# Attention outputs of two sets of tokens, instead of two partial sums, in the row halves of a tile

## The chip, the cores and the metric

The kernel runs on one core of a Trainium2 chip. The metric is the device time of one launch in microseconds (us), as the median of several runs. The engines of the core run side by side, each through its own instructions in order: TensorE (PE) for matmuls and transposes, VectorE (DVE), ScalarE (ACT), GpSimd (POOL), and SyncE (SP), which here only issues DMAs.

## The reference

One decoder layer runs over a prompt of 2048 tokens and, with the same weights, over 32 sample tokens. All is float32; the model has 1024 channels, 8 attention heads of 64 channels and as many channels (512) in a spatial gate.

```python
q, k, v, u, vg = _project(x, norm1_g, w_in)            # RMSNorm, one projection
for (w, d), bias_hj in zip(BRANCHES, biases):          # (128,1), (512,4), (2048,16)
    o, l = _dilated_prompt(q, k, v, bias_hj, d, w // d + 1)
    outs.append(o); lses.append(l)
att = _merge_branches(outs, lses).reshape(B, S, D_ATT) # softmax over the branches' sums
...
x = x + jnp.concatenate([att, u * gate], axis=-1) @ w_out
x = x + _swiglu(x, norm2_g, w_gate, w_up, w_down)      # RMSNorm, SwiGLU
```

A query sees keys at distances 0 to 128, at multiples of 4 up to 512, and at multiples of 16 up to 2048, each with a bias by distance; the three results are weighted per token and head by their softmax sums. Outputs are the new hidden states (after one more RMSNorm) and the key, value and gate caches.

## The kernel before

**Stages.** From the start of the span: the first projection with the gate and the sample's attention (to about 600 us), the prompt's attention head by head (600 to 960), a tail in which the last head's end meets the output projection of the first block (950 to 1100), then the feed-forward part for three blocks of 6, 6 and 4 token tiles of 128, of which each begins with its output projection and second norm (blocks 1 and 2 near 1640 and 2240).

**A head.** The first two branches are one banded attention: 16 query tiles, each against up to five key tiles (`band_scores`, L864; minimum and bias on DVE, L870; exp on ACT, L875; transposes, L891). Four query tiles are a group G. `band_values` multiplies the group's weights with the values. For each of the up to eight key tiles one matmul serves all query tiles that see it, up to 512 columns; an output has only the head's 64 channels, so matmuls go in turn to the upper and the lower 64 rows of a PSUM bank. Upper and lower rows thus hold two partial sums of the same tokens. `band_out` copies them to `ob` (128 x 512). The third branch works on tokens of equal remainder mod 16, four remainders at a time: POOL puts k and the two parts of q in that order (`strided_order`, L937), scores L945, softmax L950 to L960, transposes L965, values L974 (64 rows, 128 columns per remainder) and copies to `o3` (L981).

**Statistics and merge.** `Stats` turns the minima and sums of a head into two factors per token (L998 to L1028, small DVE operations and a matmul, L1004) and stores them to DRAM (`f_d`). `merge_load` brings a chunk of 512 tokens of both factors to all partitions. `merge` then multiplies the band result by the first factor (L1054), the strided one by the second (L1056) and adds the strided one to the upper rows (L1058); there are four chunks per head, nearly all on POOL, one on DVE. `merge_store` writes the upper rows to `cat_d` and the lower rows to a second place of it.

**Output projection.** `load_cat` loads a token tile: eight slices of 128 channels (gate and first partial sums) and four slices of second partial sums. `split_cat` adds the two (L1335) and splits the result in a rounded part (ACT, L1338) and the rest (DVE, L1339); `out_part` multiplies both with split weights (L1347 to L1349, 12 matmuls per half unit). `second_end` adds the last half to the residual and starts the second norm: `norm2_a` squares, `norm2_b` makes the root and the normalised tile (L1400), `norm2_c` transposes it (L1414, eight transposes into two PSUM tiles) and copies out rounded parts, rests and sums of quarters (L1422 to L1434), the operands of the feed-forward products (L1553 to L1555).

**Order of the work.** Every engine runs in the order in which the program is written. In attention a `Plan` table of steps and phases sets it. From the output projection on there are ticks: a half unit (12 matmuls) or a product is one tick, and `later(n, f)` calls `f` n ticks on. `norm2_b` comes two ticks after `norm2_a`, `norm2_c` three ticks plus `put_off` after that.

Of the kernel before, what the change touches and what calls it, by code (L numbers as in the profile page):

```python
# [19 lines left out]
P = 128  # L20
T = 2048
# [43 lines left out]
def hymba_step(ctx: ExitStack, tc: tile.TileContext, A: dict, O: dict):  # L65
# [46 lines left out]
    cat_d = dram.tile([D + DA, T], F32, name="cat_d")  # L112
# [791 lines left out]
    def band_values(it, part):  # L904

        grp, d, G = it["grp"], it["d"], it["n"] // 4
        if part == 0:
            grp["o"] = bank(3)
        o = grp["o"]
        order = [i for i in (4, 3, 5, 2, 6, 1, 7, 0) if 4 * G - 4 + i >= 0]  # L910
        L = len(order)
        for x in range(part * L // 2, (part + 1) * L // 2):
            i = order[x]
            j0, j1 = max(0, i - 4), min(3, i)
            rows = slice(x % 2 * C, x % 2 * C + C)
            pe.matmul(o[rows, j0 * P:(j1 + 1) * P].rearrange("p (a b) -> p a b", b=P), d["vb"][:, 4 * G - 4 + i, d["z"], :],
                      grp["p"][:, 16 - 4 * i + 5 * j0:16 - 4 * i + 5 * j1 + 1:5, :], start=(x < 2), stop=(x >= L - 2))

    def band_out(it):
# [3 lines left out]
        dst, o = obs[h][:, G * 512:(G + 1) * 512], it["grp"]["o"]  # L923
        if G == 0:

            pool.memset(dst[C:P, 0:P], 0.0)
            act.activation(dst[0:C], o[0:C], AF.Copy)
            act.activation(dst[C:P, P:512], o[C:P, P:512], AF.Copy)
        else:
            act.activation(dst, o, AF.Copy)  # L930
# [38 lines left out]
    def strided_values(it):  # L969
        d, r4 = it["d"], it["n"]  # L970
        it["o"] = o = bank(3)
        for a in (0, 2, 1, 3):
            sl = slice(a * P, (a + 1) * P)
            pe.matmul(o[a // 2 * C:a // 2 * C + C, sl], d["vp"][:, r4 * 4 + a, d["z"], :], it["eT"][:, sl], start=True, stop=True)  # L974

    def strided_out(it):
        r4, h = it["n"], it["h"]
        if r4 == 0:
            o3s[h] = rp.tile([P, NT, P], F32, name="o3", tag="wide", bufs=2)
        for z in range(2):  # L980
            act.activation(o3s[h][0:C, r4 * 4 + z * 2:r4 * 4 + z * 2 + 2, :],  # L981
                           it["o"][z * C:(z + 1) * C, z * 256:(z + 1) * 256].rearrange("p (r i) -> p r i", r=2), AF.Copy)
# [54 lines left out]
    def merge_load(h, ch):  # L1037

        if h < H - 2 or h == H - 2 and ch < 2:
            f = pair_tile(F32)  # L1040
            mf[h, ch] = (f[:, 0], f[:, 1])
            act.dma_start(f, dap(f_d, h * 2 * T + ch * 512, [[0, P], [T, 2], [1, 512]]))
            return
        mf[h, ch] = (raw_tile(), zn_tile())
        for z, t_ in enumerate(mf[h, ch]):
            sync.dma_start(t_, dap(f_d, (h * 2 + z) * T + ch * 512, [[0, P], [1, 512]]))

    def merge(h, ch, eng, part=None):
        f1, f3 = mf[h, ch]
        x = obs[h][:, ch * 512:(ch + 1) * 512]  # L1050
        y = o3s[h][0:C].rearrange("p r i -> p i r")[:, ch * 32:(ch + 1) * 32, :]
        by_token = lambda v: v[0:C].rearrange("p (i r) -> p i r", r=NT)
# [7 lines left out]
    def merge_store(h, c0, c1):  # L1060
        for z in range(2):
            r0 = DA * (z + 1) + h * C
            sync.dma_start(cat_d[r0:r0 + C, c0 * 512:c1 * 512], obs[h][z * C:(z + 1) * C, c0 * 512:c1 * 512])
# [257 lines left out]
    def load_cat(B, i, a, b, place=None):  # L1321
# [4 lines left out]
        m = max(a, 4)  # L1326
        for dst, r0, n in ((cl[:, a:b], a * P, b - a), (ch[:, m:b], D + (m - 4) * P, b - m)):
            sync.dma_start(dst.bitcast(F32), cat_d[r0:r0 + n * P, t0:t0 + P].rearrange("(s p) t -> p s t", p=P))
        B.late[i] = (ch, cl, a, b)

    def split_cat(B, i, staged=raw_tile):
        ch, cl, a, b = B.late.pop(i)
        m = max(a, 4)
        x = staged()[:, 0:(b - m) * P].rearrange("p (s t) -> p s t", t=P)
        dve.tensor_add(x, cl[:, m:b].bitcast(F32), ch[:, m:b].bitcast(F32))  # L1335
# [715 lines left out]
```

## Time and profile before

| | |
|---|---|
| median of 3 runs | 2692.8 us (2679.7 to 2697.14) |
| profiled execution | 2691.25 us, span 2689.5 us, mean granted clock 0.967 |
| busy share of the span | PE 94%, DVE 51%, ACT 45%, POOL 52% |
| DMA | 468.45 MB, mean 174 GB/s |
| PE busy 800 to 850 us (a stretch of heads) | 44.03 us of 50 |
| PE busy 880 to 948 us (the last head) | 58.55 of 68 |
| PE busy 948 to 1000 us (the tail) | 36.94 of 52, granted clock 0.80 |

A line of the profile has a place in the code (L916), an engine, an operation and the tiles it writes and reads; what stands behind `<-` after an idle time is the instruction that ended it. "x8" joins eight instructions that follow each other; a float32 matmul counts twice, as it passes its columns twice. PEld is the loading of a matmul's stationary operand.

### The profile page before, as it was taken

To read this page: it belongs to the slowest core of one execution; us is meant where nothing else is said; L and a number is where in the kernel's file an instruction comes from. 1 tells how busy PE (TensorE), PEld (TensorE's weight loads), DVE (VectorE), ACT (ScalarE), POOL (GpSimd) and SP (SyncE) were. 2 spreads that over 40 slices of the span, in tenths; PEclk is the share of its full clock that TensorE was granted. 3 is DMA by queue.
4 is the path that set the end of the run, shared out by engine and by line. 5 is a ranking of instruction groups with operands and counts; after the bars stand their busy time and mean duration, and the time that the engine had idled before them with its cause. 6 is when DMAs were issued, how large, how long until landed. Compare 5 with 4: busy or idle time off the path is not lost. (4 is left out here: it accounts for less than half of the span.)

```text
span 2689.5 us, 38648 instructions
## 1 busy us (share of the span) xinstructions
PE 2533.0 (94%) x13578; PEld 2170.3 (81%) x13578; DVE 1375.7 (51%) x2724; ACT 1206.2 (45%) x2569; POOL 1408.6 (52%) x1048
## 2 busy tenths in 40 slices
PE   8998999999898877999999999999999998999997
PEld 6777777676665656999999987999999987999996
DVE  3268784436666664444444465444444455444445
ACT  6423344436666636545454545433232335433333
POOL 1036553224868753767676743545363533666663
PEclk9999999999999988899999999899999999899998
DMA  8765854675556374446364554436364543555653
GB/s 245 218 201 153 258 142 134 183 252 178 171 165 201 100 209 133 141 140 205 129 200 153 176 180 153 161 129 219 126 206 147 193 158 122 172 202 197 205 198 114
DMA packets 298165, 468.45 MB, mean 174 GB/s; under 512 B 26839, under 2 KB 163208, under 8 KB 292084
## 3 DMA queue, kind: packets, MB, share of 16 engines
q1 hardware_dynamic: 283588, 443.31, 51.4%
q10 hardware_dynamic: 14384, 22.68, 3.2%
q8 instruction: 108, 1.77, 0.3%
q14 instruction: 85, 0.70, 0.1%
HBM read 374.38 MB, written 161.64 MB: 199 GB/s over the span
## 5 line engine op out<-in xcount | busy, mean ns | idle before, releaser
L1496 POOL TENSOR_TENSOR op<-fr,op 128x512 fp32r<-128x512 f32 x385 | 489.1, 1300 | 318.5 <-ACT op L1492 297.2
L1553 PE MATMUL ps_m<-xh,op 128*128 128x384 f32 (+4 forms) x1932 | 629.6, 326 | 8.4 <-ACT xh L1430 5.3
L1554 PE MATMUL ps_m<-xl,op 128*128 128x384 f32 (+4 forms) x1932 | 627.8, 325 | 7.0 <-DVE xl L1433 7.0
L1555 PE MATMUL ps_m<-xh,op 128*128 128x384 f32 (+4 forms) x1932 | 627.5, 325 | 0.0
L1626 PE MATMUL ps_o<-dw,hw 128*128 128x512 f32 x2040 | 484.1, 392 | 9.3 <-DVE acc L1628 9.3
L1626 PEld LDWEIGHTS ps_o<-dw,hw 128*128 128x128 f32 x2040 | 379.7, 188 | 91.6 <-DVE acc L1628 16.0
L1553 PEld LDWEIGHTS ps_m<-xh,op 128*128 128x128 f32 x1932 | 377.4, 195 | 13.6 <-ACT xh L1430 5.9
L1554 PEld LDWEIGHTS ps_m<-xl,op 128*128 128x128 f32 x1932 | 377.9, 196 | 11.7 <-DVE xl L1433 7.7
L1555 PEld LDWEIGHTS ps_m<-xh,op 128*128 128x128 f32 x1932 | 377.1, 195 | 0.0
L1628 DVE TENSOR_TENSOR acc<-acc,ps_o 128x512 f32<-128x512 f32 (+1 forms) x362 | 247.0, 686 | 213.8 <-PE ps_o L1626 213.7
L1593 ACT ACTIVATE ps_t<-zn 128x384 f32<-128x384 f32 (+1 forms) x126 | 58.3, 463 | 480.5 <-DVE zn L1576 371.0
L1492 ACT ACTIVATE op<-fr 128x512 fp32r<-128x512 f32 x396 | 235.8, 622 | 21.1 <-DMA fr<-ab_d 17.7
L137 POOL TENSOR_TENSOR dw<-fd,dw 128x1024 fp32r<-128x1024 f32 x66 | 158.7, 2405 | 123.4 <-ACT dw L134 123.4
L317 PE MATMUL ps_s<-wh,xh 128*128 128x512 f32 x480 | 197.7, 412 | 6.4 <-ACT xh L134 6.1
L318 PE MATMUL ps_s<-wl,xh 128*128 128x512 f32 x480 | 191.9, 400 | 0.8 <-DVE wl L225 0.8
L319 PE MATMUL ps_s<-wh,xl 128*128 128x512 f32 x480 | 191.5, 399 | 0.0
L1496 POOL TENSOR_TENSOR op<-pair,op 128x512 fp32r<-128x512 f32 x63 | 81.4, 1298 | 117.3 <-ACT op L1492 117.3
L1603 ACT ACTIVATE hw<-ps_t 128x384 fp32r<-128x384 f32 (+1 forms) x126 | 56.1, 453 | 176.7 <-DVE ps_t L1599 175.8
L317 PEld LDWEIGHTS ps_s<-wh,xh 128*128 128x128 f32 x480 | 92.7, 193 | 36.2 <-issue 8.2
L603 POOL TENSOR_TENSOR vl<-kv,vh 100x512 fp32r<-100x512 f32 (+1 forms) x32 | 45.6, 1426 | 124.1 <-ACT vh L597 41.7
L319 PEld LDWEIGHTS ps_s<-wh,xl 128*128 128x128 f32 x480 | 92.5, 193 | 20.7 <-DVE xl L137 0.2
L318 PEld LDWEIGHTS ps_s<-wl,xh 128*128 128x128 f32 x480 | 93.1, 194 | 19.3 <-DVE wl L225 2.0
(451 smaller groups left out, 4575.5 us busy)
## 6 DMA issues: line engine op xcount, KB each, us to landing
fr<-ab_d SPq DMA_DIRECT2D x308, 256.0 KB
fd<-in_w_down_dram SPq DMA_DIRECT2D x66, 512.0 KB
out_ks_dram<-in_cache_k_dram SPq DMA_DIRECT2D x56, 512.0 KB
out_vs_dram<-in_cache_v_dram SPq DMA_DIRECT2D x56, 512.0 KB
ab_d<-fr SPq DMA_DIRECT2D x88, 256.0 KB
raw<-in_w_in_dram SPq DMA_DIRECT2D x72, 256.0 KB
qk_d<-pair SPq DMA_DIRECT2D x64, 256.0 KB
ab_d<-pair SPq DMA_DIRECT2D x63, 256.0 KB
```

The lines of the kernel that those rows point to most:

```text
L137: (eng_lo or pool).tensor_sub(lo, src, hi.bitcast(F32))
L317: pe.matmul(o[j], xh[:, k, :], wh, start=(k == 0), stop=False)
L318: pe.matmul(o[j], xh[:, k, :], wl, start=False, stop=False)
L319: pe.matmul(o[j], xl[:, k, :], wh, start=False, stop=(k == KD - 1))
L1492: act.activation(ops[f, j][0], ab[f][j], AF.Copy)
L1496: (pool if f or j in POOL_LOW else dve).tensor_sub(lo_, ab[f][j], hi.bitcast(F32))
L1553: pe.matmul(out, wh[:, ks], xh[:, :, k], start=(k == 0), stop=False)
L1554: pe.matmul(out, wh[:, ks], xl[:, :, k], start=False, stop=False)
L1555: pe.matmul(out, wl[:, ks], xh[:, :, k], start=False, stop=(k == 3))
L1593: act.activation(g, c, AF.Silu)
L1626: pe.matmul(ps[0:nr], l_, r_[:, cs], start=(z == 0 and y == 0), stop=(z == FC - 1 and y == len(pairs) - 1))
L1628: dve.tensor_add(B.acc[i][0:nr, cs], B.acc[i][0:nr, cs], ps[0:nr])
```

## The change

Row halves now hold two sets of tokens. In every group of 512 tokens the upper 64 rows hold the first 256, the lower 64 rows the other 256, both complete sums.

- `band_values`: each half has its own sequence of key tiles, at most two query tiles (256 columns) per matmul; 12 matmuls per group instead of 8 (6 instead of 4 in the first group). `band_out` is one copy of 128 x 256.
- `strided_values`: each remainder's 128 columns go as two matmuls of 64 columns, read in runs of 16, to the two halves; one copy of 128 x 256 instead of two of 64 x 256.
- `merge_load`: each factor of a chunk is one DMA of half the bytes, so that each half of the partitions gets its own 256 tokens; ACT issues two where it issued one.
- `merge` works on 128 x 256 in all three operations. `merge_store` writes each token once.
- `load_cat` loads eight slices; `split_cat` has no addition, one copy and one subtraction.
- `norm2_c` copies the first PSUM tile out first; its ticks after `norm2_b` are now two by default (3 before), three for tile 2 of the first block (4 before), and one for tiles 4 and 5 of the first block and the last three tiles of the other blocks.

TensorE in a head, at the two parts of a first group's values. Before; `ps_o` is the PSUM bank, `pt` the turned weights, `ve` the values:

```order
L916 MATMUL ps_o_5981<-pt,ve 64x512
L916 MATMUL ps_o_5981<-pt,ve 64x384
L864 MATMUL ps_s<-k,qh 128x384
L864 MATMUL ps_s<-k,qh 128x256
L864 MATMUL ps_s<-k,ql 128x384
L864 MATMUL ps_s<-k,ql 128x256
L891 MATMUL ps_t_5992<-ident,e 128x128 x3
L891 MATMUL ps_o_5997<-ident,e 128x128 x2
L916 MATMUL ps_o_5981<-pt,ve 64x256
L916 MATMUL ps_o_5981<-pt,ve 64x128
```

The same place in the changed kernel:

```order
L918 MATMUL ps_o_6007<-pt,ve 64x256 x2
L918 MATMUL ps_o_6007<-pt,ve 64x128
L918 MATMUL ps_o_6007<-pt,ve 64x256
L864 MATMUL ps_s<-k,qh 128x384
L864 MATMUL ps_s<-k,qh 128x256
L864 MATMUL ps_s<-k,ql 128x384
L864 MATMUL ps_s<-k,ql 128x256
L891 MATMUL ps_t_6020<-ident,e 128x128 x3
L891 MATMUL ps_o_6025<-ident,e 128x128 x2
L918 MATMUL ps_o_6007<-pt,ve 64x256
L918 MATMUL ps_o_6007<-pt,ve 64x128
```

The matmuls stand between the same scores and transposes; those of over 256 columns have become two.

POOL in a head, where merges, casts for the strided scores (`sq`) and a subtraction of minima (`e`) follow each other. Before:

```order
L1056 TENSOR_TENSOR o_5643<-o_5643,pair 64x32x16
L953 TENSOR_TENSOR e_6081<-e_6081,st 128x512
L1058 TENSOR_TENSOR ob<-ob,o_5643 64x512
L1054 TENSOR_TENSOR ob<-ob,pair 128x512
L937 COPY sq<-k 128x512
L937 COPY sq<-qh 128x512
L937 COPY sq<-ql 128x512
```

After:

```order
L1053 TENSOR_TENSOR o_5651<-o_5651,pair 128x16x16
L949 TENSOR_TENSOR e_6110<-e_6110,st 128x512
L1055 TENSOR_TENSOR ob<-ob,o_5651 128x256
L1051 TENSOR_TENSOR ob<-ob,pair 128x256
L933 COPY sq<-k 128x512
L933 COPY sq<-qh 128x512
L933 COPY sq<-ql 128x512
```

The order is kept, the merge's operations have half as many elements per partition.

TensorE in block 1, where the output projection ends and the products begin. Before: the transposes of the fourth tile (`ps_t`) stand between the last matmuls of the projection and the first product, which needs that tile:

```order
L1347 MATMUL ps_o_15602<-wol,xh_14891 128x512
L1348 MATMUL ps_o_15602<-wol,xh_14891 128x512
L1349 MATMUL ps_o_15602<-wol,xl_14892 128x512
L1414 MATMUL ps_t_15663<-ident,pair 128x128 x4
L1414 MATMUL ps_t_15668<-ident,pair 128x128 x4
L1553 MATMUL ps_m_15691<-xh_14891,op 128x256
L1554 MATMUL ps_m_15691<-xl_14892,op 128x256
L1555 MATMUL ps_m_15691<-xh_14891,op 128x256
```

After, the fourth tile's transposes stand two half units earlier, ahead of the last tile's projection (`ps_o_15782`):

```order
L1338 MATMUL ps_o_15721<-wol,xh_15076 128x512
L1339 MATMUL ps_o_15721<-wol,xh_15076 128x512
L1340 MATMUL ps_o_15721<-wol,xl_15077 128x512
L1405 MATMUL ps_t_15783<-ident,pair 128x128 x4
L1405 MATMUL ps_t_15788<-ident,pair 128x128 x4
L1338 MATMUL ps_o_15782<-woh,xh_15076 128x512
L1339 MATMUL ps_o_15782<-woh,xh_15076 128x512
L1340 MATMUL ps_o_15782<-woh,xl_15077 128x512
```

It is the fifth tile's transposes that now stand directly ahead of the first product, which reads the first four tiles only; the last tile's stand two products after it, where the fifth tile's stood before.

The diff, without repeated context:

```diff
...
-    cat_d = dram.tile([D + DA, T], F32, name="cat_d")
+    cat_d = dram.tile([D, T], F32, name="cat_d")
     f_d = dram.tile([H, 2, T], F32, name="f_d")
...
         o = grp["o"]
-        order = [i for i in (4, 3, 5, 2, 6, 1, 7, 0) if 4 * G - 4 + i >= 0]
-        L = len(order)
+        seqs = [[i for i in s if 4 * G - 4 + i >= 0] for s in ((4, 3, 0, 2, 1, 5), (4, 3, 2, 5, 6, 7))]
+        L = max(len(s) for s in seqs)
         for x in range(part * L // 2, (part + 1) * L // 2):
-            i = order[x]
-            j0, j1 = max(0, i - 4), min(3, i)
-            rows = slice(x % 2 * C, x % 2 * C + C)
-            pe.matmul(o[rows, j0 * P:(j1 + 1) * P].rearrange("p (a b) -> p a b", b=P), d["vb"][:, 4 * G - 4 + i, d["z"], :],
-                      grp["p"][:, 16 - 4 * i + 5 * j0:16 - 4 * i + 5 * j1 + 1:5, :], start=(x < 2), stop=(x >= L - 2))
+            for z, seq in enumerate(seqs):
+                if x >= len(seq):
+                    continue
+                i = seq[x]
+                j0, j1 = max(2 * z, i - 4), min(2 * z + 1, i)
+                pe.matmul(o[z * C:(z + 1) * C, (j0 - 2 * z) * P:(j1 - 2 * z + 1) * P].rearrange("p (a b) -> p a b", b=P),
+                          d["vb"][:, 4 * G - 4 + i, d["z"], :],
+                          grp["p"][:, 16 - 4 * i + 5 * j0:16 - 4 * i + 5 * j1 + 1:5, :], start=(x == 0), stop=(x == len(seq) - 1))
     def band_out(it):
...
             obs[h] = lo.tile([P, T], F32, name="ob", tag="ob", bufs=2)
-        dst, o = obs[h][:, G * 512:(G + 1) * 512], it["grp"]["o"]
-        if G == 0:
-
-            pool.memset(dst[C:P, 0:P], 0.0)
-            act.activation(dst[0:C], o[0:C], AF.Copy)
-            act.activation(dst[C:P, P:512], o[C:P, P:512], AF.Copy)
-        else:
-            act.activation(dst, o, AF.Copy)
+        act.activation(obs[h][:, G * 256:(G + 1) * 256], it["grp"]["o"][:, 0:256], AF.Copy)
     def strided_order(h, r4):
...
     def strided_values(it):
...
         it["o"] = o = bank(3)
-        for a in (0, 2, 1, 3):
-            sl = slice(a * P, (a + 1) * P)
-            pe.matmul(o[a // 2 * C:a // 2 * C + C, sl], d["vp"][:, r4 * 4 + a, d["z"], :], it["eT"][:, sl], start=True, stop=True)
+        for a in range(4):
+            for z in range(2):
+                pe.matmul(o[z * C:(z + 1) * C, a * C:(a + 1) * C].rearrange("p (b w) -> p b w", w=NT),
+                          d["vp"][:, r4 * 4 + a, d["z"], :],
+                          it["eT"][:, a * P:(a + 1) * P].rearrange("p (b z w) -> p z b w", z=2, w=NT)[:, z],
+                          start=True, stop=True)
     def strided_out(it):
...
         if r4 == 0:
-            o3s[h] = rp.tile([P, NT, P], F32, name="o3", tag="wide", bufs=2)
-        for z in range(2):
-            act.activation(o3s[h][0:C, r4 * 4 + z * 2:r4 * 4 + z * 2 + 2, :],
-                           it["o"][z * C:(z + 1) * C, z * 256:(z + 1) * 256].rearrange("p (r i) -> p r i", r=2), AF.Copy)
+            o3s[h] = rp.tile([P, NT, P], F32, name="o3", tag="wide", bufs=2)[:, :, 0:C]
+        act.activation(o3s[h][:, r4 * 4:r4 * 4 + 4, :], it["o"][:, 0:256].rearrange("p (r i) -> p r i", r=4), AF.Copy)
...
             f = pair_tile(F32)
-            mf[h, ch] = (f[:, 0], f[:, 1])
-            act.dma_start(f, dap(f_d, h * 2 * T + ch * 512, [[0, P], [T, 2], [1, 512]]))
-            return
-        mf[h, ch] = (raw_tile(), zn_tile())
+            mf[h, ch] = tuple(f[:, z, 0:256] for z in range(2))
+        else:
+            mf[h, ch] = tuple(t_[:, 0:256] for t_ in (raw_tile(), zn_tile()))
         for z, t_ in enumerate(mf[h, ch]):
-            sync.dma_start(t_, dap(f_d, (h * 2 + z) * T + ch * 512, [[0, P], [1, 512]]))
+            (act if h < H - 2 or h == H - 2 and ch < 2 else sync).dma_start(
+                t_, dap(f_d, (h * 2 + z) * T + ch * 512, [[256, 2], [0, C], [1, 256]]))
     def merge(h, ch, eng, part=None):
         f1, f3 = mf[h, ch]
-        x = obs[h][:, ch * 512:(ch + 1) * 512]
-        y = o3s[h][0:C].rearrange("p r i -> p i r")[:, ch * 32:(ch + 1) * 32, :]
-        by_token = lambda v: v[0:C].rearrange("p (i r) -> p i r", r=NT)
+        x = obs[h][:, ch * 256:(ch + 1) * 256]
+        y = o3s[h].rearrange("p r i -> p i r")[:, ch * 16:(ch + 1) * 16, :]
+        by_token = lambda v: v.rearrange("p (i r) -> p i r", r=NT)
         if part in (None, 0):
...
     def merge_store(h, c0, c1):
+        r0 = DA + h * C
         for z in range(2):
-            r0 = DA * (z + 1) + h * C
-            sync.dma_start(cat_d[r0:r0 + C, c0 * 512:c1 * 512], obs[h][z * C:(z + 1) * C, c0 * 512:c1 * 512])
+            sync.dma_start(cat_d[r0:r0 + C, c0 * 512:c1 * 512].rearrange("p (c z w) -> p c z w", z=2, w=256)[:, :, z],
+                           obs[h][z * C:(z + 1) * C, c0 * 256:c1 * 256].rearrange("p (c w) -> p c w", w=256))
...
             B.cat[i, s] = (ch[:, s], cl[:, s])
-        m = max(a, 4)
-        for dst, r0, n in ((cl[:, a:b], a * P, b - a), (ch[:, m:b], D + (m - 4) * P, b - m)):
-            sync.dma_start(dst.bitcast(F32), cat_d[r0:r0 + n * P, t0:t0 + P].rearrange("(s p) t -> p s t", p=P))
+        sync.dma_start(cl[:, a:b].bitcast(F32), cat_d[a * P:b * P, t0:t0 + P].rearrange("(s p) t -> p s t", p=P))
         B.late[i] = (ch, cl, a, b)
-    def split_cat(B, i, staged=raw_tile):
+    def split_cat(B, i):
         ch, cl, a, b = B.late.pop(i)
-        m = max(a, 4)
-        x = staged()[:, 0:(b - m) * P].rearrange("p (s t) -> p s t", t=P)
-        dve.tensor_add(x, cl[:, m:b].bitcast(F32), ch[:, m:b].bitcast(F32))
-        for y0, y1, src in ((a, m, cl[:, a:m].bitcast(F32)), (m, b, x)):
-            if y0 < y1:
-                act.activation(ch[:, y0:y1], src, AF.Copy)
-                dve.tensor_sub(cl[:, y0:y1], src, ch[:, y0:y1].bitcast(F32))
+        act.activation(ch[:, a:b], cl[:, a:b].bitcast(F32), AF.Copy)
+        dve.tensor_sub(cl[:, a:b], cl[:, a:b].bitcast(F32), ch[:, a:b].bitcast(F32))
     def out_part(B, i, half, ss, ps, start, stop):
...
-            later(3 + put_off, norm2_c, B, i, xn)
+            later(put_off, norm2_c, B, i, xn)
     def norm2_c(B, i, xn):
...
         def sums_of():
-            act.activation(t4, b12, AF.Copy)
             dve.tensor_sub(t1, t4, b11)
...
             act.activation(at_(hi, 0, 1)[:, 0], b11, AF.Copy)
+            act.activation(t4, b12, AF.Copy)
+            dve.tensor_sub(at_(lo_, 0, 1)[:, 0], b11, at_(hi, 0, 1)[:, 0].bitcast(F32))
             act.activation(at_(hi, 1, 3), pts[1], AF.Copy)
             sums_of()
-            dve.tensor_sub(at_(lo_, 0, 1)[:, 0], b11, at_(hi, 0, 1)[:, 0].bitcast(F32))
             dve.tensor_sub(at_(lo_, 1, 3), pts[1], at_(hi, 1, 3).bitcast(F32))
...
         else:
+            act.activation(t4, b12, AF.Copy)
             sums_of()
...
     at(L - 3, "misc", lambda: load_cat(B, 0, 0, 7, first_place()))
-    at(L + 1, "misc", split_cat, B, 0, lambda: ap_.tile([P, 512], F32, name="m0", tag="m0", bufs=1))
+    at(L + 1, "misc", split_cat, B, 0)
     for j, ss in enumerate(((0, 1), (2,), (3,), (4, 5), (6,))):
...
-    def second_end(B, i, ps, put_off=0):
+    def second_end(B, i, ps, put_off=2):
         out_end(B, i, 1, ps)
...
         open_end(B, 2)
-        second_end(B, 2, p2, 1)
+        second_end(B, 2, p2, 3)
         p1 = second_unit(B, 1)
...
         for i in (4, 5):
-            second_end(B, i, second_unit(B, i))
+            second_end(B, i, second_unit(B, i), 1)
     def first_end(B, i):
...
         for i in order:
-            second_end(B, i, second_unit(B, i))
+            second_end(B, i, second_unit(B, i), 1 if i in tiles[-3:] else 2)
         if B.last:
...
```

## The prediction

> **What bounds the kernel now.** I read the page first, then TensorE's waits, then the two stages that the change touches by windows, then single waits on the timeline.
>
> ```profile
> span 2689.5 us, 38648 instructions
> ```
>
> The profiled execution took 2691.25 us, 1.55 below the median of 2692.8. TensorE is the bound almost throughout, so only what TensorE waits for can be won. Its waits in the stages concerned (total, times, longest):
>
> ```profile
> PE ps_s L864 <- DVE st L870: 16.7, 13, 3.9
> PE ps_s L945 <- POOL sq L937: 13.2, 20, 2.1
> ...
> PE ps_t L1414 <- DVE xl L1433: 7.8, 6, 2.6
> PE ps_m L1554 <- DVE xl L1433: 7.0, 3, 2.7
> ...
> PE ps_m L1553 <- ACT xh L1430: 5.3, 2, 2.9
> ...
> PE ps_s L945 <- DVE e L950: 3.5, 2, 3.3
> ...
> PE ps_t L1414 <- DVE xl L137: 3.0, 2, 2.6
> ```
>
> The first, second and sixth row belong to attention, the others to the second norm. The windows are a steady stretch of heads, the last head, and the tail, where the last merges meet the out-projection. Columns: length, then busy time and count of PE, weight loads, DVE, ACT and POOL, granted clock, DMA share, GB/s.
>
> ```profile
> 800.00:850.00 50.00, 44.03 (x299) 31.14 (x299) 32.33 (x75) 30.90 (x76) 37.78 (x33) 0.97 0.62 179
> ...
> 880.00:948.00 68.00, 58.55 (x401) 42.14 (x399) 46.74 (x92) 44.42 (x104) 56.62 (x50) 0.95 0.41 108
> 948.00:1000.00 52.00, 36.94 (x150) 25.56 (x151) 33.25 (x56) 17.24 (x37) 28.52 (x19) 0.80 0.71 186
> ```
>
> In a steady head PE idles about 6 us of 50, in the last head 9.5 of 68, in the tail 15 of 52 and at clock 0.80. So the tail has the most to give.
>
> **TensorE's own work.** A band group now (two parts), a strided group, the 64-column matmuls of an earlier stage, and 16-column matmuls on 128-column weights (each f32 matmul is two passes, so x8 is four instructions):
>
> ```profile
> 677.71 1.73 PE L916 MATMUL ps_o<-pt,ve 128*64 128x512 f32 x8
> ```
> ```profile
> 680.69 0.87 PE L916 MATMUL ps_o<-pt,ve 128*64 128x256 f32 x8
> ```
> ```profile
> 684.29 0.66 PE L974 MATMUL ps_o<-eT,v 128*64 128x128 f32 x8
> ```
> ```profile
> 267.83 1.05 PE L453 MATMUL ps_t<-pair,wbd 32*32 32x64 f32 x16 [4.01 <-issue]
> ```
> ```profile
> 781.12 0.62 PE L1004 MATMUL ps_o<-sel_r,sm 128*128 128x16 f32 x4
> ```
>
> Upper and lower row halves go at the same time. The wide part has 512+384 columns in each half, 1792 column passes; the narrow one 256+128, 768 passes. (1.73−0.87)/1024 = 0.84 ns per pass, 0.23 us fixed. After, each part has 256+256+128 columns per half: 1280 passes, 1.30 us, so the group takes 2.61 instead of 2.60: nothing. The first group of a head goes from 768 to 896 columns in its longer half: 256 passes, +0.21 us, ×8 heads = **+1.7**. A strided group has 2×128 columns per half before and 4×64 after: 512 passes both times, 0.66 us. In the 64-column row (1.05−0.23)/16 = 51 ns a pass is 0.80 ns per column, so issuing them is not the limit. But weights change twice as often: by the last row a load of 128 columns paces at (0.62−0.23)/4 = 0.10 us, so 64 columns at some 0.05, just the length of a 64-column pass. If such loads, or a moving operand read in runs of 16, which no row shows, cost the double, it is +0.43 us × 32 = +13.8; a gain is excluded, since the column count stays. I take 0, the 64-column row being nearest.
>
> **POOL, ACT and DVE in the heads.**
>
> ```profile
> L1056 POOL TENSOR_TENSOR o<-o,pair 64x512 f32<-64x512 f32 x26 | 41.8, 1607 | 0.0
> ...
> L1058 POOL TENSOR_TENSOR ob<-ob,o 64x512 f32<-64x512 f32 x25 | 38.5, 1539 | 1.3
> ...
> L1054 POOL TENSOR_TENSOR ob<-ob,pair 128x512 f32<-128x512 f32 x26 | 34.1, 1312 | 5.7 <-DMA pair<-f_d 5.6
> ...
> L981 ACT ACTIVATE o<-ps_o 64x256 f32<-64x256 f32 x64 | 24.1, 377 | 3.6 <-PE ps_o L974 3.1
> ...
> L930 ACT ACTIVATE ob<-ps_o 128x512 f32<-128x512 f32 x21 | 12.4, 592 | 7.1 <-PE ps_o L916 7.1
> ```
> ```profile
> L137 POOL TENSOR_TENSOR dw<-fd,dw 128x1024 fp32r<-128x1024 f32 x66 | 158.7, 2405 | 123.4 <-ACT dw L134 123.4
> ```
>
> A merge of a chunk is 1.31+1.61+1.54 = 4.46 us on POOL. 512 more elements cost 2.405−1.312 = 1.09 us, so 256 fewer save 0.55, at least that for the strided two too: I take 0.55+0.7+0.7 = 1.95 per chunk, 7.8 per head of four chunks, 60 over 31 POOL chunks; bounds 1.6 and 2.2. Who waits for it:
>
> ```profile
> 674.97 1.61 POOL L1056 TENSOR_TENSOR o<-o,pair 64x512 f32<-64x512 f32 x1
> ...
> 683.57 1.07 POOL L937 CAST sq<-k 128x512 fp32r<-128x512 f32 x1
> ...
> 685.58 1.05 POOL L937 CAST sq<-ql 128x512 fp32r<-128x512 f32 x1
> ```
>
> From 674.97 POOL works without a pause through five merge instructions to the casts at 683.57, for which the strided scores (L945) wait. Five halved instructions come 3.2 us sooner, more than the longest steady wait of that kind; so of the 13.2 us nearly all can go. ACT loses one copy in two (32×0.377 = 12.1 us) and a third of the band copy-outs, and issues 26 more DMAs (the factors now come in two); it is busy 31 of 50 us and no wait above is for it, so I count nothing. Late next is DVE: its two-input instructions meet POOL (below) and then hold the band scores, the 16.7 us. I take it that the 2.8 us of the last head apart, 10.4 of the POOL waits go, 5 of them come back as DVE waits in the same head, and 3 of the DVE waits go with POOL's load: **−8** (−3 to −14).
>
> The last head has the other 2.8 us of POOL waits, 3.3 for e, and POOL busy 56.6 of 68 us with some seven chunks, 14 us less after: **−6** (−2 to −9).
>
> **The tail.** TensorE's waits, with what DVE and POOL did:
>
> ```profile
> 951.74 0.90 PE L864 MATMUL ps_s<-k,qh 128*128 128x384 f32 x2 [3.86 <-DVE st L870]
> ...
> 966.00 1.01 PE L1004 MATMUL ps_t<-sel_r,sm 128*128 128x16 f32 x4 [3.37 <-DVE sm L998]
> ...
> 988.83 0.57 PE L1347 MATMUL ps_m<-op,accm 128*128 128x512 f32 x1 [2.84 <-ACT accm L1338]
> ...
> 992.63 0.79 PE L1349 MATMUL ps_m<-op,accm 128*128 128x512 f32 x1 [2.81 <-DVE accm L1339]
> ```
> ```profile
> 943.28 4.48 DVE L1014 TENSOR_TENSOR f<-s,st 64x16 f32<-64x16 f32 x1
> ...
> 958.03 1.40 DVE L1335 TENSOR_TENSOR m<-pair 128x384 f32<-128x384 f32 x1
> ```
> ```profile
> 981.80 1.29 POOL L1054 TENSOR_TENSOR ob<-ob,raw 128x512 f32<-128x512 f32 x1 [7.81 <-DMA raw<-f_d]
> ```
>
> Before 951.74 DVE stood 4.48 us in a 16-element operation while POOL ran two merge and two split instructions; two of the four halve, some 1.3, and less queues behind them: −1.5. Before 966.00 DVE adds the partial sums (L1335, 1.40, gone) and merges a chunk (halved, some 0.8): −2.4. The last pair waits for a loaded tile whose split begins with L1335, and for loads at a full DMA; each tile loads 512 KB instead of 768, a chunk's factors halve: −4. Two shorter waits of the same kind: −1. Of the clock lost at 0.80, if it reaches 0.87, 36.94×(1−0.80/0.87) = 3 us: −3. Sum **−12** (−5 to −21; the low end if POOL's wait of 7.81 for the factors' DMA, which is a chain of a store and a load, sets the time).
>
> The clock part goes by this row: a band group after no wait over 1 us, at half rate (3.10 against 1.73):
>
> ```profile
> 778.09 3.10 PE L916 MATMUL ps_o<-pt,v 128*64 128x512 f32 x8
> ```
>
> The Trainium skill, "TensorE: Matmul & The Clock Gate", Part 1, has the clock fall only after an idle window of some 3.4 us. The row disagrees; by the rule the clock would come back only where 3.86 and 3.37 go. By it the −3 would be about −1.5 and the sum 1.5 higher.
>
> **The second norm.** The transposes now precede one or two half units of out-projection more. Block 1, before; then DVE's and ACT's part:
>
> ```profile
> 1679.22 0.58 PE L1553 MATMUL ps_m<-xh,op 128*128 128x256 f32 x1 [2.89 <-ACT xh L1430]
> 1681.95 0.58 PE L1554 MATMUL ps_m<-xl,op 128*128 128x256 f32 x1 [2.15 <-DVE xl L1433]
> ...
> 1686.34 1.04 PE L1414 MATMUL ps_t<-ident,pair 128*128 128x128 f32 x8
> ```
> ```profile
> 1676.14 0.16 DVE L141 RECIPROCAL s<-s 128x1 f32<-128x1 f32 x1 [0.27 <-ACT s L1369]
> ```
> ```profile
> 1677.14 1.15 ACT L1400 ACTIVATE pair<-acc,s 128x1024 f32<-128x1024 f32 x1 [1.03 <-DVE s L145]
> ...
> 1678.81 0.36 ACT L1430 ACTIVATE xh<-ps_t 128x256 fp32r<-128x256 f32 x1
> ...
> 1681.14 1.15 ACT L134 ACTIVATE xh<-zn 128x512 fp32r<-128x512 f32 x2 [1.21 <-DVE zn L1425]
> ```
>
> The waits of the first products (5.3+7.0 = 12.3 us, three blocks) go, since two half units lie between. Of the transposes' waits for a bank (7.8+3.0 = 10.8) the earlier copy-out takes some 4.8. Against that the last transposes come one tick after the normalised tile is ordered: 1676.14 to 1678.29 makes it 2.15 us, behind another tile's copy-out on ACT (1678.81 to 1682.29, 3.5), while TensorE has one product, (1686.34−1681.95)/2 = 2.2: a wait of 3.4, and 0.4 where a half unit lies between, less 0.4 by the new order: 3.4 per block, +10.2. Sum −12.3−4.8+10.2 = **−7** (−15 to +5).
>
> **Sum.** 1.7−8−6−12−7 = −31.3, 2691.25−31.3 = **2660**.
>
> **Rivals.**
> (A) The forecast, 0.50; its own range 2648 to 2676.
> (B) What goes comes back: DVE's waits replace POOL's (heads −3, last head −3), the factors' DMA chain holds the tail (−5), and the waits for the normalised tile eat all of the norm's gain (0): 1.7−11 = −9, 2682. For it: L864's waits on DVE are already the largest, and 7.81 is a DMA wait. Against: POOL has no pause before the casts. Chance 0.33.
> (C) More: waits and clock both go, at the favourable ends of the heads, the last head and the tail: 1.7−14−9−21−7 = −49, 2642. For it: clock 0.80 in the tail. Chance 0.10.
> (D) Slower. The two row halves no longer run together: their weights are now loaded 12 times per group and half where it was 8, each for half the columns, and a load that is not covered stops both. Run in turn, a full band group takes 5120 column passes where it took 2560: +2560×0.84 = 2.15 us × 24 groups = 52; a first group +1024×0.84 = 0.86 × 8 = 7; a strided one +0.43 × 32 = 14. With the other terms (−33): +73−33 = +40, 2731. It decides from 33/73 = 45% of the overlap lost. Against it: today's rows show the halves together, with passes as narrow as 128. Chance 0.07.
> The Trainium skill, "TensorEngine Tiling (Array Packing)", section "Instruction Overhead", speaks against narrow matmuls: some 60 cycles each at the least, so a small dimension is not to be split. No row here has passes of under 64 columns bound by issue alone; by the rule 64 is just above the edge and the price 0.
>
> That the change does not do what it says is excluded for sizes and places, which its order of instructions shows.
>
> **Chances and range.** One per cent is 26.9 us, about what a measurement of this kernel can tell from no change: that makes faster below 2665.9, and slower above 2719.7. Faster: 0.45 of A's 0.50 and C's 0.10; same: the rest of A, all of B; slower: most of D. So 0.55, 0.39, 0.06. The range 2638 to 2688 leaves out D and the edges of B and C.
>
> **What would show it.** L1051, L1053 and L1055 (the merge) near 0.75, 0.9 and 0.85 us; L941's waits for POOL under 3 us; a band part at 1.30 us, a strided group at 0.66; 948 to 1000 shorter by a quarter with a clock above 0.85; no waits of the first products but some at L1405 for ACT. Wrong would be: band parts of 2 us (D); L864's waits for DVE above 20 us, or L1405's above 20 (B).

## The result, and the profile after

The changed kernel takes 2672.9 us (median of 9 runs, 2667.1 to 2676.1), the kernel before 2692.8 (2679.7 to 2697.1). The ratio is 0.9925, 95% interval 0.991 to 0.994: 20 us faster, less than 1%. The profiled execution of the changed kernel took 2675.66 us with a span of 2673.9; against the profiled execution of before that is 15.6 us. The prediction had 2660, a gain of 31.

TensorE's largest waits outside the first stage, in the changed kernel (total, times, longest):

```profile
PE ps_t L1405 <- ACT pair L1391: 13.4, 6, 4.6
...
PE ps_s L864 <- DVE st L870: 8.3, 7, 1.9
PE ps_t L1338 <- ACT accm L1329: 7.1, 1, 7.1
PE ps_t L961 <- ACT e L952: 6.7, 8, 1.6
...
PE ps_m L1338 <- ACT accm L1329: 5.2, 1, 5.2
...
PE ps_s L941 <- POOL sq L933: 4.3, 5, 1.7
```

The waits for POOL's casts went from 13.2 to 4.3 and those for DVE's band statistics from 16.7 to 8.3, and no wait of the first products is left. But the waits for two loaded tiles of the output projection are 7.1 and 5.2 us, where the same tiles cost 2.1 (the two rows below, of before) and 5.7 (2.84 and 2.81) before, and the transposes of the second norm now wait 13.4 us for the normalised tile.

```profile
977.55 0.50 PE L1347 MATMUL ps_t<-op,accm 128*128 128x512 f32 x1 [1.17 <-ACT accm L1338]
...
979.20 0.79 PE L1349 MATMUL ps_t<-op,accm 128*128 128x512 f32 x1 [0.92 <-DVE accm L1339]
```

Where the 15.6 us arise, by stage. The marks are TensorE instructions that both kernels have: the first matmul of the prompt's head statistics, the first output-projection matmul of each block, the last matmul.

| stage (us) | before | changed | difference |
|---|---|---|---|
| heads: first statistics to block 0's projection | 312.3 | 304.9 | -7.4 |
| block 0: to block 1's projection (with the tail) | 645.0 | 642.4 | -2.6 |
| block 1: to block 2's projection | 606.1 | 598.1 | -8.0 |
| block 2: to the end | 459.4 | 463.7 | +4.3 |

The other 2 us lie ahead of the heads and behind the last matmul. The heads' windows, before and after (length, busy time and count of PE, weight loads, DVE, ACT, POOL, granted clock, DMA share, GB/s):

```profile
648.20:960.50 312.30, 271.21 (x1840) 194.03 (x1839) 209.16 (x471) 203.17 (x492) 239.22 (x205) 0.96 0.54 155
```
```profile
647.10:952.00 304.90, 271.72 (x2255) 217.73 (x2254) 196.69 (x470) 182.12 (x457) 187.18 (x198) 0.94 0.40 124
```

POOL has 52 us less to do, and TensorE gets only 7 of them; its clock went from 0.96 to 0.94 (a second profiled execution of the changed kernel, listed below with the two ticks, had the heads at 301.0 us and 0.96). TensorE's and POOL's own instructions came out as priced:

```profile
683.48 1.30 PE L918 MATMUL ps_o<-pt,ve 128*64 128x256 f32 x12
...
687.29 0.69 PE L970 MATMUL ps_o<-eT,v 128*64 128x64 f32 x16
```
```profile
L1053 POOL TENSOR_TENSOR o<-o,pair 128x256 f32<-128x256 f32 x26 | 24.5, 941 | 19.2 <-DMA pair<-f_d 13.8 <-ACT pt L896 3.2 <-ACT e L875 2.3
...
L1055 POOL TENSOR_TENSOR ob<-ob,o 128x256 f32<-128x256 f32 x26 | 22.6, 868 | 1.3
...
L1051 POOL TENSOR_TENSOR ob<-ob,pair 128x256 f32<-128x256 f32 x26 | 19.1, 733 | 4.5 <-DMA pair<-f_d 4.4
```

A band part is 1.30 us as worked out, a strided group 0.69 against 0.66 forecast, a merge 0.73+0.94+0.87 = 2.54 instead of 4.46. New is that POOL's merges wait 18 us for the DMA that brings the factors, where they waited 5.6.

**What the factors' loads do.** In the tail POOL shows it most plainly:

```profile
959.57 0.73 POOL L1051 TENSOR_TENSOR ob<-ob,raw 128x256 f32<-128x256 f32 x1 [9.04 <-DMA raw<-f_d]
962.51 0.90 POOL L1053 TENSOR_TENSOR o<-o,zn 128x256 f32<-128x256 f32 x1 [2.21 <-DMA zn<-f_d]
...
965.45 0.74 POOL L1051 TENSOR_TENSOR ob<-ob,raw 128x256 f32<-128x256 f32 x1 [1.12 <-DMA raw<-f_d]
968.37 0.87 POOL L1053 TENSOR_TENSOR o<-o,zn 128x256 f32<-128x256 f32 x1 [2.17 <-DMA zn<-f_d]
```

Each of four loads arrives 2.9 us after the one before. They are 128 KB each; a stretch in which nothing else is loaded gives the rate:

```profile
949.50:954.50 5.00, 4.38 (x32) 2.78 (x28) 1.97 (x5) 3.18 (x8) 0.95 (x2) 1.00 0.13 44
...
958.00:963.00 5.00, 5.00 (x26) 3.31 (x25) 2.52 (x11) 0.72 (x2) 1.22 (x2) 0.66 0.15 48
```

The DMA share is 0.13 to 0.15 of 16 engines, about two of them, at 44 to 48 GB/s: 128 KB take some 2.8 us. The changed load's source pattern begins with the two token sets, `[[256, 2], [0, C], [1, 256]]`; before it began with 128 (`[[0, P], [T, 2], [1, 512]]`). The Trainium skill, "DMA: Bandwidth & Descriptors", section "Rules for kernel authors", says that an outermost dimension of fewer than 16 confines a whole DMA to at most that many of the 16 engines. The share of 2/16 agrees.

The loads also hold the engine that issues them, first ACT in a head, at four in a row:

```profile
657.69 4.15 ACTq L1042 DMA_DIRECT2D pair<-f_d  x3
...
661.89 0.49 ACT L896 ACTIVATE pt<-ps_t 128x384 f32<-128x384 f32 x1 [4.27 <-PE ps_s L864]
```

The copy of the turned weights (L896), queued behind the issues on ACT, starts 4.27 us after ACT's last work and 0.05 after the last issue ends. The profile puts the idle time down to TensorE, but the transposes that this copy reads were over at 659.27, 2.6 us before it:

```profile
658.78 0.49 PE L891 MATMUL ps_t<-ident,e 128*128 128x128 f32 x3
```

### The profile page after: what moved, and what is told of

It is laid out like the page before. It is cut to its first block, busy times and chain, and to the rows that moved or that the text cites. A ratio compares the mean times of both kernels' runs of the same rounds, so it can differ in the third digit from the quotient of the medians.

```text
span 2673.9 us, 39478 instructions
## 1 busy us (share of the span) xinstructions
PE 2528.4 (95%) x14058; PEld 2194.8 (82%) x14058; DVE 1341.9 (50%) x2691; ACT 1179.1 (44%) x2513; POOL 1348.5 (50%) x1040
## 4 chain that ended last, share of the span: by engine, by line
PE 53%; POOL 8%; issue 7%; ACT 4%; DMA 4%; DVE 4%; SPq 1%; ACTq 1%; POOLq 0%; DVEq 0%
PE ps_o L1618 12%; PE ps_m L1545 8%; PE ps_m L1547 8%; PE ps_m L1546 8%; POOL op L1488 2%; DMA ab_d<-pair 2%; PE ps_o L918 2%; ACT fr L1456 1%; PE ps_s L864 1%; PE ps_s L941 1%; PE ps_t L891 1%; ACTq L1042 1%; POOL pair L1468 1%; POOL fr L1471 1%; POOL dw L137 1%
## 5 line engine op out<-in xcount | busy, mean ns | idle before, releaser
L1545 PE MATMUL ps_m<-xh,op 128*128 128x384 f32 (+4 forms) x1932 | 626.1, 324 | 0.0
L1545 PEld LDWEIGHTS ps_m<-xh,op 128*128 128x128 f32 x1932 | 374.6, 194 | 4.2
```

The costliest lines, as they stand in the source:

```text
L1545: pe.matmul(out, wh[:, ks], xh[:, :, k], start=(k == 0), stop=False)
```

## The experiments

Each run stands beside runs of the kernel before on the same chip. Differences between kernels of different chips are taken by their ratios to that.

**The second norm's part alone, and attention's part alone.** The first is the kernel before with the new `norm2_c` and the new ticks; the second the changed kernel with the old ones, of which this is the core:

```diff
-            later(put_off, norm2_c, B, i, xn)
+            later(3 + put_off, norm2_c, B, i, xn)
...
-            second_end(B, i, second_unit(B, i), 1 if i in tiles[-3:] else 2)
+            second_end(B, i, second_unit(B, i))
```

> The kernel before with only the second norm's part of the change (order of the copies out, transposes sooner). If that part earns what the trace of the changed kernel shows from the first block's projection to its end (about 8 us in block 0, 7 in block 1, minus 3 in block 2), this is 9 to 14 us faster than before, about 2680. If the prediction's sum for it is right it is 7 faster. If it only moves waits that a later attention would have hidden, it stays within 3 us of before.

> The changed kernel with the second norm as before. If the parts add up, this is 5 to 10 us faster than before (changed kernel minus the second norm's 11). By the prediction's sum for attention and tail alone it would be 24 us faster. In the tail between 950 and 1000 us the loads of the factors should again land one after the other, some 3 us apart.

Measured: the norm alone 2686.3 us, 0.9964 (0.9938 to 0.9991) of before; attention alone 2686.2, 0.9985 (0.9971 to 0.9998). So the parts are worth 10 and 4 us by the ratios (5 and 5 by the medians), and 14 together (11) against 20 for the whole: by the ratios they add within the intervals, which are wide. The norm alone spreads from 2664 to 2690 us: three of its ten executions lie at 2664 to 2669 with a mean granted clock of 0.975 or 0.976, the others at 2677 to 2690 with 0.965 to 0.969. Its profiled execution is the shortest, so that isn't used for stages. In the tail of attention alone the factors' loads land some 3 us apart again, as expected. Attention's part by stages: heads 305.4, block 0 649.2, block 1 605.9, block 2 456.1. Against before, heads gain 6.9 and block 0 loses 4.2. Against the changed kernel, which differs from it in the norm alone, the norm is worth 6.8 in block 0, 7.8 in block 1, and costs 7.6 in block 2.

**The factors' loads cut the other way.** Two loads per chunk as in the change, of the same bytes, but each brings both factors to 64 partitions:

```diff
-            f = pair_tile(F32)
-            mf[h, ch] = tuple(f[:, z, 0:256] for z in range(2))
+            f = pair_tile(F32)[:, :, 0:256]
         else:
-            mf[h, ch] = tuple(t_[:, 0:256] for t_ in (raw_tile(), zn_tile()))
-        for z, t_ in enumerate(mf[h, ch]):
-            (...).dma_start(t_, dap(f_d, (h * 2 + z) * T + ch * 512, [[256, 2], [0, C], [1, 256]]))
+            f = raw_tile().rearrange("p (z w) -> p z w", z=2)
+        mf[h, ch] = tuple(f[:, z] for z in range(2))
+        for z in range(2):
+            (...).dma_start(f[z * C:(z + 1) * C], dap(f_d, h * 2 * T + ch * 512 + z * 256, [[0, C], [T, 2], [1, 256]]))
```

> The changed kernel, but the two loads of a chunk's factors are cut by row halves (64 partitions, both factors) instead of by factor (both halves, one factor). Same bytes, same number of loads. Theory: a load whose outermost dimension is 2 is spread over two of the sixteen DMA engines only (2.2 busy engines in the packets of those loads) and takes 2.7 us for 128 KB, which holds ACT and SyncE when several are queued, and times the tail. Then each load takes under 1.5 us, TensorE's waits of 7.1 and 5.2 us in the tail fall by 8 to 12 in all, the heads lose some of their waits on ACT too, and the kernel is 8 to 14 us faster than the changed one (2660). Rival: the tail hangs on the chain of storing, loading and splitting as such, whatever the loads' shape: then no change (within 3 us).

Measured: 2637.6 us, 0.9806 (0.9776 to 0.9835) of before, 54 us faster than before and some 32 faster than the changed kernel, over twice what was expected. Heads 283.4 (changed 304.9), block 0 627.6 (642.4), blocks 1 and 2 as changed (597.7, 463.1). Its heads by windows, a burst of four issues on ACT, and TensorE's waits for DVE, for the casts and for a tile of the tail:

```profile
651.80:935.20 283.40, 260.59 (x2256) 208.91 (x2255) 197.88 (x470) 181.81 (x457) 187.13 (x198) 0.98 0.44 135
```
```profile
661.97 2.66 ACTq L1042 DMA_DIRECT2D pair<-f_d  x4
```
```profile
PE ps_s L864 <- DVE st L870: 9.6, 8, 1.8
...
PE ps_s L941 <- POOL sq L933: 3.7, 4, 1.8
...
PE ps_t L1338 <- ACT accm L1329: 3.2, 1, 3.2
```

Four issues take 2.66 us, no longer 4.8 (0.62 and 4.15). ACT and POOL are as busy as in the changed kernel (181.8 and 187.1); what changed is when they come.

**The loads' shape in the kernel before.** All else as before, the same values to all 128 partitions, but in a pattern that begins with 2, in one load per factor (so ACT issues two per chunk here too):

```diff
-            act.dma_start(f, dap(f_d, h * 2 * T + ch * 512, [[0, P], [T, 2], [1, 512]]))
+            for z in range(2):
+                act.dma_start(f[:, z], dap(f_d, (h * 2 + z) * T + ch * 512, [[0, 2], [0, C], [1, 512]]))
...
-            sync.dma_start(t_, dap(f_d, (h * 2 + z) * T + ch * 512, [[0, P], [1, 512]]))
+            sync.dma_start(t_, dap(f_d, (h * 2 + z) * T + ch * 512, [[0, 2], [0, C], [1, 512]]))
```

> The kernel before, with the factors loaded by a source pattern whose outermost dimension is 2 (the same values to all partitions, same bytes, two loads per chunk). Theory of the two engines: 256 KB per load at 49 KB per us is 5.2 us each, 10.5 per chunk; the last six chunks of the tail need 63 us of it, and the kernel is slower than before by 15 to 50 us. Rival (the shape is without effect): within 3 us of before.

Measured: 2866.6 us, 1.0658 (1.0636 to 1.0681): 175 us slower, far above the expected 15 to 50, which counted the tail alone; the heads lose most, 146 us (458.0 against 312.3). A stretch in which nothing else is loaded, and who waits for the loads:

```profile
660.00:665.00 5.00, 2.71 (x17) 1.67 (x15) 1.17 (x3) 0.00 (x0) 3.24 (x4) 1.00 0.13 51
```
```profile
  POOL o L1057: 64.8, 16
  POOL ob L1055: 60.6, 16
  ACT pt L896: 59.7, 6
```

Again 0.13, two of sixteen, and 51 GB/s. With twice the bytes of the changed kernel, POOL waits 125 us for the loads and ACT 60 behind them. With the run before, this settles the shape as the cause: it takes the gain away where it is put in, and gives it where it is taken out.

**Two ticks instead of one for the late transposes,** in all blocks, then in the last block alone, both on the kernel with row-half loads:

```diff
-            second_end(B, i, second_unit(B, i), 1)
+            second_end(B, i, second_unit(B, i))
...
-            second_end(B, i, second_unit(B, i), 1 if i in tiles[-3:] else 2)
+            second_end(B, i, second_unit(B, i))
```
```diff
-            second_end(B, i, second_unit(B, i), 1 if i in tiles[-3:] else 2)
+            second_end(B, i, second_unit(B, i), 1 if i in tiles[-3:] and not B.last else 2)
```

> The kernel with loads cut by row halves, and all late tiles' transposes two ticks after their normalised tile instead of one. TensorE's six waits of the transposes for ACT's normalised tile (16.0 us there) should go, but the last tile's operands come later. If those waits are the price that the prediction gave (3.4 us per block), this is 3 to 10 us faster than the kernel with one tick (2637.6). Rival: they only stand in for the first products' waits, which come back: within 4 us.

> The kernel with loads cut by row halves, with two ticks instead of one in the last block alone, whose transition was 3 to 4 us longer in the changed kernel's trace than before, at a granted clock of 0.67 and 0.56. If a wait of 2 us for the normalised tile brings that clock down, this is 4 to 8 us faster than the kernel with one tick (2637.6); if the clock falls there whatever stands in front, within 3 us.

Measured: 2630.3 us, 0.976 (0.9733 to 0.9787), and 2629.0, 0.9765 (0.9728 to 0.9801). Both intervals overlap that of one tick on another chip, so one tick, two ticks in all blocks and the changed kernel were set side by side.

> The kernel with loads cut by row halves once more, as the base for the next two on the same chip: 2634 to 2642, 1.8 to 2.1% faster than before.

> Two ticks for all late tiles, beside the one above on the same chip. By the stages of the two profiled executions (block 1 from projection to projection 4.8 us shorter, block 2 2.5 shorter) it is 5 to 10 us faster than with one tick. Rival: the two were within their spread, and the difference is under 3 us.

> The changed kernel itself on the same chip as the two above: 2668 to 2676, some 35 us slower than with loads cut by row halves.

Measured on one chip: one tick 2636.7 us, 0.9791 (0.9772 to 0.9811); two ticks 2632.3, 0.9775 (0.9756 to 0.9794); the changed kernel 2674.5, 0.993 (0.9909 to 0.995). The row-half loads are confirmed at 38 us. Two ticks are 4 us better in the median, less than the expected 5 to 10, and the intervals overlap: inconclusive. In the first run with two ticks the waits for the normalised tile are 8.8 us, with one tick 16.0: 7 us less waiting, of which the medians show 4. One wait of a first product comes back for it (2.8 us, at L1545).

**POOL's work put back.** The kernel with row-half loads, and three more multiplications of 128x256 on POOL per chunk, first into the unused half of the factors' tile, then from the band result into a tile of their own:

```diff
+        def more(f1):
+            if sp is not None:
+                pool.tensor_mul(sp, f1, f1)      # after each of the three operations
```
```diff
+        def more():
+            if eng is pool and h < H - 1:        # ahead of each of the three operations
+                pool.tensor_mul(spare, obs[h][:, ch * 256:(ch + 1) * 256], obs[h][:, ch * 256:(ch + 1) * 256])
```

> The kernel with loads cut by row halves, with three more POOL multiplications of 128x256 per chunk into an unused half of the factors' tile, 26 chunks: POOL is about as busy with merges as before the change (some 57 us more in the heads). If POOL's shorter queue is what the heads gained by, TensorE's waits for the casts and for DVE come back and the kernel is 10 to 20 us slower than without (2650 to 2658). If the gain came from ACT's and DVE's shorter work or from the loads, under 4 us slower.

> As the run with more POOL multiplications, but these read the band result and write a tile of their own, so that they hold no tile that a load waits for; 84 of them, each in front of one of a chunk's three operations. In the run before, ACT waited some 20 us for POOL to release the factors' tile, which the kernel before did not do. If POOL's queue alone accounts for the heads' gain, the kernel is again 20 to 30 us slower than without (2657 to 2667); if that run's loss was ACT's wait for the tile, under 12 us (below 2649).

Measured: 2667.7 us, 0.9901 (0.9879 to 0.9923), slower than expected, and 2664.3, 0.9886 (0.9837 to 0.9936), as expected of POOL's queue. The heads take 310.3 and 303.8 us instead of 283.4, the other stages are within 2 us. In the first of the two, ACT waits for POOL to let go of the factors' tile, which is an effect of the experiment:

```profile
L875 ACT ACTIVATE e<-e,st 128x640 f32<-128x640 f32 (+2 forms) x107 | 80.6, 755 | 19.0 <-POOL pair L1054 12.5 <-DVE st L870 6.5
```

So the second counts. Its heads, and its wait for the casts:

```profile
652.90:956.70 303.80, 267.92 (x2255) 213.06 (x2254) 198.55 (x470) 182.37 (x457) 233.35 (x278) 0.96 0.41 125
```
```profile
PE ps_s L941 <- POOL sq L933: 18.0, 22, 1.9
```

With 46 us more of POOL work TensorE waits 18.0 us for the casts instead of 3.7, and its clock is 0.96 again instead of 0.98. DVE is as busy as without it (198.6 against 197.9), and its waits hold TensorE no longer than before (10.0 us at L864, against 9.6). So 20 of the 29 us that the heads gain with good loads go again when POOL's work alone comes back: 13 of them are idle time of TensorE, 5 the clock (both worked out as in the second table below). The rest is not split further; fewer copies on ACT and smaller loads are in it.

## Why the prediction was right or wrong

The forecast of a gain was right, and 2672.9 lies in the range; it was 11 us short of the gain forecast. That the total came so near is luck in good part: errors of opposite sign made it up. Terms of the sum, against the stages:

| term | forecast | changed | loads by row halves |
|---|---|---|---|
| TensorE's own work, heads, last head | +1.7 -8 -6 = -12.3 | -7.4 | -28.9 |
| tail | -12 | +4 | -11 |
| second norm | -7 | -7 | -8 |
| the rest of blocks 1 and 2 | 0 | -3.5 | -3 |
| sum | -31.3 | -14 | -51 |

The tail is block 0 with the old norm against before, 649.2 and 634.0 against 645.0 (634.0 is attention's part alone with row-half loads, below); the norm is the difference to that kernel over three blocks. The heads end here with block 0's first projection, 960.5 us before, so the first 12 us of the prediction's tail, with its wait of 3.86, count with the heads.

> Attention's part of the change alone, with loads cut by row halves; second norm as before. If parts add, 5 to 11 us slower than with the second norm's part (2637.6), so 2643 to 2649, and some 40 faster than attention's part with the loads as changed (2686.2).

Measured: 2646.2 us, 0.9822 (0.9797 to 0.9847). By stages 283.1, 634.0, 606.2, 456.2. The norm on top of it is worth 6.4 and 8.5 us in blocks 0 and 1 and costs 6.9 in block 2.

The sum has the clock in one place alone, -3 in the tail. The same stages by TensorE's idle time and by what it lost to the clock, which is the length of a stretch times what its granted clock is short of 1, added up over the trace's clock records (idle / clock, us):

| stage | before | attention alone | changed | changed, row-half loads |
|---|---|---|---|---|
| heads | 41.1 / 13.7 | 32.3 / 20.5 | 33.2 / 18.8 | 22.8 / 6.8 |
| block 0 | 32.8 / 23.9 | 37.2 / 25.6 | 35.9 / 17.1 | 25.4 / 10.2 |
| block 1 | 7.5 / 11.9 | 7.4 / 11.9 | 6.6 / 5.1 | 6.6 / 5.1 |
| block 2 | 11.1 / 13.7 | 8.0 / 15.4 | 6.1 / 23.9 | 8.9 / 20.5 |

Point by point:

- **The step that failed: the price of the loads.** The prediction counted nothing for the 26 more issues on ACT, "no wait above is for it", and took "a chunk's factors halve" as a gain in the tail. It priced the loads by bytes and by the duration of an issue, not by the pattern's outermost dimension, which stood in the diff. The loads take 2.8 us each on two engines; in the heads that costs 21.5 us (304.9 against 283.4), in the tail 15 (642.4 against 627.6); between the two profiled executions on one chip it is 17.6 and 13.9. The tail's rival condition in the range, that the wait for the factors' DMA sets the time, is what happened, for a reason that was not named; the tail's +4 lies outside even that end of its range, -5.
- **Mis-sized: the heads.** The mechanism was right (casts sooner, DVE less held), but with good loads it is 28.9 us and not 12.3. The step "5 of them come back as DVE waits" failed: with row-half loads the DVE waits fall too, from 16.7 to 9.6 us, and TensorE's busy time falls by 10.6 us (271.2 to 260.6). The clock, which goes from 0.96 to 0.98, makes 7 of these by the table; the other 4 are not accounted for. The prediction had counted no clock in the heads. Idle time makes up the other 18.3 (41.1 to 22.8). The loads and the heads are errors of opposite sign and hid each other in the total.
- **Right: TensorE's own passes.** 1.30 us per part, 0.69 per strided group; 64-column passes and reads in runs of 16 are covered. So the slower rival (the two halves no longer together) did not occur.
- **The second norm: the sum right by luck.** It is -7 against -7, and the waits moved as told: the first products no longer wait, the last transposes wait 13.4 us (forecast 10.2). But the blocks were to gain alike, and instead blocks 0 and 1 gain 6.8 and 7.8 us and block 2 loses 7.6. Between attention alone and the changed kernel TensorE's idle time falls by only 0.8 to 1.9 us in each block; the loss to the clock falls by 8.5 and 6.8 and rises by 8.5. The waits in the sum thus were not what set the blocks' times; the clock, at nothing in this term, was. Windows around the last projections of block 1 (two rows) and block 2 (two rows), before and after:

```profile
1650.00:1690.00 40.00, 34.71 (x185) 29.40 (x183) 21.81 (x67) 22.32 (x48) 13.07 (x10) 0.91 0.14 42
1690.00:1725.00 35.00, 33.80 (x190) 33.27 (x190) 11.78 (x32) 16.34 (x33) 20.84 (x16) 0.76 0.42 138
...
2255.00:2285.00 30.00, 24.34 (x144) 21.58 (x143) 14.13 (x50) 16.36 (x38) 7.58 (x6) 0.83 0.03 9
2285.00:2312.00 27.00, 25.98 (x154) 25.86 (x154) 9.32 (x32) 11.20 (x28) 14.68 (x11) 0.68 0.34 110
```
```profile
1639.00:1676.00 37.00, 31.24 (x163) 26.23 (x162) 22.43 (x68) 22.94 (x49) 15.14 (x12) 0.94 0.12 43
1676.00:1706.40 30.40, 30.40 (x212) 30.40 (x212) 12.32 (x30) 15.34 (x30) 17.12 (x13) 0.91 0.42 141
...
2236.00:2263.00 27.00, 22.77 (x104) 20.60 (x105) 14.09 (x48) 15.51 (x36) 9.67 (x8) 0.67 0.00 1
2263.00:2297.00 34.00, 34.00 (x174) 34.00 (x174) 7.16 (x27) 10.16 (x26) 12.98 (x10) 0.56 0.29 94
```

In block 1 the clock is higher after, in block 2 lower: there TensorE idles less, but the clock is 0.67 and 0.56 instead of 0.83 and 0.68, over 60 us. Most of that is one piece at half rate, with TensorE busy almost throughout, and the first run with two ticks has such a piece as well:

```profile
2248.30:2292.70 44.40, 43.57 (x202) 43.08 (x203) 14.28 (x53) 17.38 (x45) 13.69 (x11) 0.50 0.18 60
```
```profile
2203.60:2248.00 44.40, 44.40 (x207) 44.21 (x208) 13.79 (x52) 17.85 (x44) 14.84 (x11) 0.50 0.18 60
```

In the second, TensorE has no wait for the normalised tile left in that block, only one of 2.8 us for an operand of a product; so the former is not what holds the clock down. Why the clock stays low so long was not settled.

- **Rival B** (the gain comes back as other waits) has the nearest time, 2682, and one of its three causes, the DMA of the factors; the heads' other waits did not replace POOL's, as the run with good loads shows. Rival C, at 2642, is near what the kernel with good loads comes to (2637), but by other terms.

## What to carry to other kernels

A DMA's cost is not its bytes alone: look at the outermost dimension of its pattern first; 64 and 128 did well here, 2 did not. A broadcast that is cut in two is better cut into loads that each begin with many partitions than into one whose first dimension is 2. And when a change of layout halves an engine's work, but the total hardly moves, compare the stretch's DMA share and the issue times of its loads before looking for a new wait among the engines. Count the clock as well: waits of TensorE of under 1 us each, close together, were paid here a second time at half rate (last rows below).

The version with row-half loads is the best of those timed against both kernels: 2636.7 us with one tick, 2632.3 with two, 2.1 to 2.25% under the kernel before.

## What the runs showed of the hardware that was not expected

- Loads of 128 KB in a pattern that begins with 2 moved at 44 to 48 GB/s with a DMA share of 0.13 to 0.15; cut by row halves the same bytes let a burst of four issues pass in 2.66 us instead of 4.8.
- An engine that issues several such loads in a row stands: the issues on ACT took 0.49 us at the least and up to 3.2 (first row below), with copies and exponentials queued behind them; in the kernel before they took 0.37 to 0.55, with row-half loads 0.58 to 1.38 (second and third row; least, median and longest in ns).

```profile
L1042 ACTq DMA_DIRECT2D pair<-f_d x52: 488/512/3179, 657.0 to 923.4; - x52
```
```profile
L1042 ACTq DMA_DIRECT2D pair<-f_d x26: 366/366/554, 657.5 to 928.1; - x26
```
```profile
L1042 ACTq DMA_DIRECT2D pair<-f_d x52: 581/617/1378, 662.0 to 909.6; - x52
```

- 46 us of additional POOL work in the heads cost 20 us in time though POOL was idle for a quarter of the stretch even then (233 busy of 304), and TensorE's clock went with it, 0.98 to 0.96. The Trainium skill, "TensorE: Matmul & The Clock Gate", Part 1, ties a fall of the clock to an idle window of some 3.4 us. Taken as one wait, this run doesn't agree, since no wait in that stretch was over 3 us, and the prediction's row of 3.10 us was read in this way (in the 3.4 us ahead of it TensorE is busy for 2.00). Taken as 3.4 us in which TensorE does little, it does: two waits for the casts, of 0.60 and 0.85 us, leave TensorE busy for 1.95 us of 3.4, and the next 3.4 us go at half rate. All six falls in these heads follow such a stretch, with TensorE busy for 59% of it at most.

```profile
779.20:782.60 3.40, 1.95 (x22) 1.67 (x17) 1.03 (x4) 1.13 (x6) 3.24 (x5) 1.00 1.02 424
782.60:786.00 3.40, 3.40 (x18) 1.86 (x16) 1.71 (x3) 1.21 (x4) 3.32 (x5) 0.50 0.21 87
```
